# Fixed places for the transpositions between the output projection and the embedding's projection, whose results VectorE now takes out of PSUM

## The chip, the cores and the metric

The kernel is one program on one NeuronCore of a Trainium2 chip. Its time is the device time of one execution in microseconds (us). Five engines run their own instruction streams: PE (TensorE, matrix products, with its weight loads shown as PEld), DVE (VectorE), ACT (ScalarE), POOL (GpSimd) and SP (SyncE, which here only starts transfers). ACT and POOL can start transfers too. An engine works through its own stream in order, and waits where an instruction needs a result of another engine.

## The reference

One layer of a hybrid transformer on 512 tokens of width 1024, in float32. Two attentions (`nsa_mixer`, `moba_mixer`) give `y_nsa` and `y_moba`; after that:

```python
merged = sigmoid(gate_a) * (y_nsa @ w_up_nsa) + sigmoid(gate_b) * (y_moba @ w_up_moba)
x = x + merged @ w_out                                   # the output projection
gate, up = split(rms_norm(x, g_ffn) @ w_ffn_in, 2)       # the first feed-forward product
x = x + (silu(gate) * up) @ w_ffn_out
ple_gate = sigmoid(rms_norm(x, g_ple) @ w_ple_gate)
x = x + ple_gate * (p @ w_ple_proj)                      # p: an embedding of width 256 per token
```

The stage in question runs from the end of `merged @ w_out` to the first blocks of the feed-forward product. The embedding's projection `p @ w_ple_proj` depends on none of this; its result is needed only in the last line.

## The kernel before

**Precision.** Each float32 operand is split into a rounded high part and a low rest: ACT copies the high part (`wh`, L114 for weights; `x..h`, L1059 for activations), DVE subtracts it to get the low part (`wl`, L115; `x..l`, L1060). Each product is three matmuls: high by high, low by high, high by low (L1013, L1015, L1016 in the helper `mm`; L1132, L1134, L1135 in `in_product`). Weights arrive through SP's queue as pieces of 128x1024 (`wr`), which are numbered in the order of their use; `wh` and `wl` have four buffers each, taken in turn, so that piece 70 overwrites piece 66, and 71 overwrites 67.

**Output projection.** Eight PSUM tiles of 128 tokens x 512 columns: token tile `tt` = 0..3, column half `n` = 0, 1. They are named `wo<n><tt>`. Half of the contraction is done for all eight first; then, tile by tile, `wo_part` adds the second half (12 matmuls) and DVE adds the tile to the residual `X2[tt]` (L1073).

**Normalization and transposition.** When both column halves of two token tiles are done, `normed` takes the mean square of each row (ACT squares with a running sum, L1023; DVE scales, L1024; POOL raises to the power -1/2, L1025) and ACT scales the rows (L1027), giving `xs0`, `xs1` for the first pair of token tiles and `xs2`, `xs3` for the second. `turned_x` transposes them on PE (L1035): for each of four values of `u`, four 128x128 transpositions into one PSUM bank (`tx`), and ACT moves the bank to SBUF in two pieces with the gain `g_ffn` (`put_b`, L1064). The results are `B[k][c]`, k the half of the width, c the pair of token tiles: `B00`, `B10` come from the first pair, `B01`, `B11` from the second.

**Feed-forward product.** It is done by seven products per block instead of eight, on sums and differences of the four quarters. The operands are `x11` = B00, `x21` = B10, `x22` = B11, and `xt1`..`xt4`, which DVE forms from all four (L1096 to L1103). A block p does its products in an order of its own; in block 0 it is x11 (into bank `fx`), x21 (`fy`), xt1 (`fz`), xt2 (`fx` again, after ACT has copied it), then xt3, x22 and xt4. The weight pieces are 68 to 74 in block 0 and 75 to 81 in block 1; pieces 71 and 73 are sums that DVE forms in place (L106), of piece 70 with 68 and of that with 69.

**Embedding's projection.** `pj_part(n)` makes four tiles per column half (`pjb`, six matmuls each, weight pieces 66 and 67). ACT copies each to SBUF (`pps`, L1089) and starts its transfer to a DRAM buffer `ppd` (L1090), from which it is read back near the end.

**What sets the order.** The code is traced in the order in which it is written, and a scheduler then puts the instructions of each engine into an order of its own by a timeline that it estimates. `tc.issue_after(i)` ties the instructions of a block behind instruction `i` on its engine. The order below is what the scheduler made. PSUM has eight banks under four tags (`s`, `v`, `a`, `b`), two each; in the stage, the projection holds all eight, and `tx`, `pjb`, `fx`, `fy` and `fz` take them over as they come free.

Of the kernel before, what the change touches and what calls it, by code (L numbers as in the profile page):

```python
# [10 lines left out]
F32 = mybir.dt.float32  # L11
F32R = mybir.dt.float32r
I32 = mybir.dt.int32
AF = mybir.ActivationFunctionType
# [182 lines left out]
def hybrid_kernel(ctx: ExitStack, tc: tile.TileContext, a, out):  # L197
# [13 lines left out]
    def t4(name, dt=F32R):  # L211
        return big.tile([128, 2, 512], dt, name=name, tag="t4")

    def flat(t):
        return t.rearrange("p a b -> p (a b)")
# [795 lines left out]
    def mm(o, b, sth, stl, mh, ml, stop):  # L1011

        T.matmul(o, sth, mh, start=b.name not in seen, stop=False, skip_group_check=True)  # L1013
        seen.add(b.name)
        T.matmul(o, sth, ml, start=False, stop=False, skip_group_check=True)  # L1015
        T.matmul(o, stl, mh, start=False, stop=stop, skip_group_check=True)  # L1016

    def normed(c, name):

# [10 lines left out]
    def turned_x(xs, tag, put, us=range(4)):  # L1030
        for u in us:
            b = bank("tx", tag)
            for j in range(2):
                for i in range(2):
                    T.transpose(b[:, j * 256 + i * 128:j * 256 + i * 128 + 128],  # L1035
                                xs[i][:, (2 * u + j) * 128:(2 * u + j) * 128 + 128], ident)
            for j in range(2):
                put(2 * u + j, b[:, j * 256:j * 256 + 256])

    wob = [four("wo0", "sv"), four("wo1", "ab")]  # L1040

    def wo_part(n, u, w, tt):
        for j in range(2):
            kt = 2 * u + j
            mh, ml = (x[:, j * 512:(j + 1) * 512] for x in w)
            mm(wob[n][tt], wob[n][tt], MH[kt][:, tts(tt)], ML[kt][:, tts(tt)], mh, ml, kt == 7)

    for n in range(2):
        for u in range(2):
# [1 line left out]
            for tt in range(QT):  # L1051
                wo_part(n, u, w, tt)
    wn = [[W.get((f"wo{n}", u)) for u in (2, 3)] for n in range(2)]
    B = [[flat(t4(f"B{k}{c}", F32)) for c in range(2)] for k in range(2)]
    op = {}

    def split_x(nm, src):
        h, l = op[nm] = [flat(t4(f"x{nm}{x}")) for x in "hl"]
        A.activation(h, src, AF.Copy)  # L1059
        V.tensor_sub(l, src, h.bitcast(F32))  # L1060

    def put_b(c):
        def put(kt, src):
            A.activation(B[kt // 4][c][:, kt % 4 * 256:kt % 4 * 256 + 256], src, AF.Copy, scale=gv[:, 1, kt:kt + 1])  # L1064
        return put

    xs = [None, None]
    for tt in range(QT):
        for n in range(2):
            for u in (2, 3):  # L1070
                wo_part(n, u, wn[n][u - 2], tt)
            x = X2[tt][:, n * 512:(n + 1) * 512]
            V.scalar_tensor_tensor(x, wob[n][tt], 0.5, x, op0=OP.mult, op1=OP.add)  # L1073
        if tt % 2:
            xs[tt // 2] = normed(tt // 2, "xs")
        if tt == 2:
            turned_x(xs[0], "b", put_b(0))
            split_x("11", B[0][0])
            split_x("21", B[1][0])

    def pj_part(n):
        w = W.get(("pj", n))
        for tt in range(QT):
            b = bank("pjb", "va"[tt % 2])
            for kt in range(2):
                mh, ml = (x[:, kt * 512:(kt + 1) * 512] for x in w)
                mm(b, b, PIh[:, kt, tts(tt)], PIl[:, kt, tts(tt)], mh, ml, kt == 1)
            t = t2("pps")
            A.activation(t, b, AF.Copy)  # L1089
            A.dma_start(ppd[tt][:, n * 512:(n + 1) * 512], t)  # L1090

    pj_part(0)
    turned_x(xs[1], "b", put_b(1))
    pj_part(1)
    t1x, t2x = (flat(t4(f"x{nm}", F32)) for nm in ("t1", "t2"))
    V.tensor_tensor(t1x, B[0][0], B[0][1], op=OP.subtract)  # L1096
    split_x("t1", t1x)
# [262 lines left out]
```

## Time and profile before

| what | value |
|---|---|
| median of 3 runs | 844.34 us (843.9 to 844.61) |
| the profiled execution's own time | 842.11 us |
| its span, first to last instruction | 840.4 us |
| mean granted TensorE clock | 0.989 |
| PE busy | 818.4 us, 97% of the span |
| DVE busy | 620.1 us, 74% |
| ACT busy | 478.8 us, 57% |
| POOL busy | 144.6 us, 17% |

The span and what lies around it differ by 1.71 us. Times in the views count from the first instruction. A row of a timeline has the start, the duration (of a merged row, from its first start to its last end), engine, line, operation, tile written<-tiles read, shape, count, and in brackets the idle time before it with the instruction that ended it. Matmuls are pipelined: the duration of one is longer than the distance to the next. The granted clock (PEclk) is given as a share of full speed.

### The profile page before, as it was taken

How to read it: one execution, taken by the hardware profiler on the slowest of the kernel's cores; microseconds unless marked ns; L12 is line 12 of the kernel's file. 1: busy time of each engine (PE TensorE's matmuls, PEld its weight loads, DVE VectorE, ACT ScalarE, POOL GpSimd, SP SyncE). 2: the span in 40 equal slices, each digit the busy share in tenths (PEclk: the TensorE clock that was granted, in tenths of full speed). 3: DMA queues.
4: the chain of work that ended last, by engine and by line, in shares of the span. 5: the costliest groups of instructions: out<-in, count | busy, mean ns of one | idle time of the engine just before them, and what ended most of it. 6: DMA issues, size and time to landing. Idle time of an engine off the chain costs nothing.

```text
span 840.4 us, 12951 instructions
## 1 busy us (share of the span) xinstructions
PE 818.4 (97%) x4875; PEld 725.6 (86%) x4875; DVE 620.1 (74%) x1049; ACT 478.8 (57%) x823; POOL 144.6 (17%) x218
## 2 busy tenths in 40 slices
PE   9989999999999999999997999999999999999997
PEld 8869898788788888788885999999999988888776
DVE  7697758788977988739527877777778899966552
ACT  7434655876776767734448554544555644846441
POOL 3864426001111211007000111111120000000000
PEclk9989999999999999999998899999999999999999
DMA  9414554317888895234614367779998256577431
GB/s 346 153 58 131 164 142 126 101 51 217 230 223 208 236 270 144 76 101 168 207 39 162 114 236 275 279 238 271 275 273 247 76 151 205 155 222 210 175 147 51
DMA packets 40543, 150.31 MB, mean 179 GB/s; under 512 B 5153, under 2 KB 5537, under 8 KB 37921
## 3 DMA queue, kind: packets, MB, share of 16 engines
q1 hardware_dynamic: 30064, 98.61, 35.5%
q0 software_dynamic: 8064, 46.14, 21.6%
q10 hardware_dynamic: 2352, 4.73, 1.8%
q8 instruction: 38, 0.62, 0.3%
q14 instruction: 25, 0.20, 0.1%
HBM read 142.13 MB, written 50.33 MB: 229 GB/s over the span
## 4 chain that ended last, share of the span: by engine, by line
PE 87%; DVE 6%; ACT 3%; DMA 1%; issue 1%; POOL 0%; SPq 0%; ACTq 0%
PE fx L1132 5%; PE fx L1134 5%; PE fx L1135 5%; PE ga L412 3%; PE pt L834 3%; PE ga L414 3%; PE ga L413 3%; PE fz L1134 3%; PE fz L1135 3%; PE fz L1132 3%; PE fs L1016 2%; PE fs L1015 2%; PE fs L1013 2%; PE pv L858 2%; PE wo L1016 2%; PE wo L1015 2%
## 5 line engine op out<-in xcount | busy, mean ns | idle before, releaser
L114 ACT ACTIVATE wh<-wr 128x1024 fp32r<-128x1024 f32 (+2 forms) x196 | 199.0, 1021 | 177.6 <-issue 53.2
L115 DVE TENSOR_TENSOR wl<-wr,wh 128x1024 fp32r<-128x1024 f32 (+2 forms) x196 | 233.2, 1200 | 73.9 <-ACT wh L114 73.6
L412 PE MATMUL ga<-xh,wh 128*128 128x512 f32 x128 | 53.5, 418 | 0.0
L809 DVE CUSTOM_DVE_ANT_0 p<-sb,big_mask 128x512 f32<-128x512 f32 (+2 forms) x96 | 44.9, 486 | 9.1 <-PE sb L807 7.9
L413 PE MATMUL ga<-xl,wh 128*128 128x512 f32 x128 | 50.3, 393 | 0.0
L414 PE MATMUL ga<-xh,wl 128*128 128x512 f32 x128 | 50.1, 393 | 0.0
L834 PE MATMUL pt<-ident,p 128*128 128x128 f32 x240 | 38.3, 273 | 1.6 <-DVE pw L844 1.3
L844 DVE TENSOR_TENSOR pw<-pt,pw 128x512 fp32r<-128x512 f32 x48 | 32.7, 684 | 7.0 <-ACT pw L843 6.8
L1176 POOL COPY mark<-ks 128x1 f32<-128x1 f32 x11 | 7.9, 718 | 173.8 <-DVE ks L1146 173.8
L843 ACT ACTIVATE pw<-pt 128x512 fp32r<-128x512 f32 x48 | 28.0, 593 | 12.2 <-PE pt L834 11.8
L834 PEld LDWEIGHTS pt<-ident,p 128*128 128x128 f32 x240 | 28.9, 140 | 6.9 <-issue 1.4
L414 PEld LDWEIGHTS ga<-xh,wl 128*128 128x128 f32 x128 | 24.0, 188 | 5.3
L1132 PE MATMUL fz<-xt1h,wh 128*128 128x256 f32 x88 | 26.1, 297 | 1.9 <-ACT xt1h L1059 1.9
L1013 PE MATMUL pgb<-wh,x3h 128*128 128x512 f32 (+1 forms) x72 | 25.6, 372 | 1.8 <-ACT wh L114 1.2
L1134 PE MATMUL fz<-xt1l,wh 128*128 128x256 f32 x88 | 26.1, 297 | 0.9 <-DVE xt1l L1060 0.9
L413 PEld LDWEIGHTS ga<-xl,wh 128*128 128x128 f32 x128 | 24.2, 189 | 3.2
L106 DVE TENSOR_TENSOR wr<-wr,wr 128x1024 f32<-128x1024 f32 x22 | 26.8, 1220 | 0.1
L412 PEld LDWEIGHTS ga<-xh,wh 128*128 128x128 f32 x128 | 24.2, 189 | 3.1
L1015 PE MATMUL pgb<-wl,x3h 128*128 128x512 f32 (+1 forms) x72 | 25.8, 368 | 0.5 <-DVE wl L115 0.5
L1135 PE MATMUL fz<-xt1h,wl 128*128 128x256 f32 x88 | 26.0, 295 | 0.0
L1016 PE MATMUL pgb<-wh,x3l 128*128 128x512 f32 (+1 forms) x72 | 25.4, 368 | 0.0
L1132 PE MATMUL fx<-xt2h,wh 128*128 128x256 f32 x88 | 25.0, 284 | 0.0
(724 smaller groups left out, 2733.1 us busy)
## 6 DMA issues: line engine op xcount, KB each, us to landing
gs<-g POOLq DMA_DIRECT2D x20, 1024.0 KB, 8.9
wr<-g SPq DMA_DIRECT2D x33, 512.0 KB, 7.0
fs<-f POOLq DMA_DIRECT2D x24, 704.0 KB, 10.1
wr<-gs SPq DMA_DIRECT2D x22, 512.0 KB, 9.5
wr<-fs SPq DMA_DIRECT2D x20, 512.0 KB, 4.4
wr<-ga SPq DMA_DIRECT2D x16, 512.0 KB, 3.5
wr<-f SPq DMA_DIRECT2D x15, 512.0 KB, 3.7
fs<-fs POOLq DMA_DIRECT2D x8, 704.0 KB, 13.4
```

What stands on the lines that cost most here:

```text
L114: self.nc.scalar.activation(h[:, a:b], t[:, a:b], AF.Copy)
L115: self.nc.vector.tensor_sub(l[:, a:b], t[:, a:b], h[:, a:b].bitcast(F32))
L412: T.matmul(o, wh[:, sl], h, start=start, stop=False)
L413: T.matmul(o, wh[:, sl], l, start=False, stop=False)
L414: T.matmul(o, wl[:, sl], h, start=False, stop=stop)
L809: V.tensor_tensor_reduce(out=p, in0=o, in1=big_mask[:, 512 - n:512], op0=OP.add, op1=OP.min, scale=1.0, scalar=3.0e38, accum_out=st["m"][: ...
L834: last = T.transpose(b[:, off:off + 128], st["p"][:, P_OFF[qt] + kb * 128:P_OFF[qt] + kb * 128 + 128], ident)
L1015: T.matmul(o, sth, ml, start=False, stop=False, skip_group_check=True)
L1016: T.matmul(o, stl, mh, start=False, stop=stop, skip_group_check=True)
L1132: T.matmul(o, wh, xh, start=b.name not in seen, stop=False, skip_group_check=True)
L1134: T.matmul(o, wh, xl, start=False, stop=False, skip_group_check=True)
L1135: T.matmul(o, wl, xh, start=False, stop=kt == 3, skip_group_check=True)
```

## The change

The first pair's transpositions are written behind tiles (tt 2, n 1) and (tt 3, n 0) of the output projection, two values of `u` at each, and each next tile of the projection is tied behind the last transposition. They use the banks of tag `a`. All of column half 0 of the embedding's projection is tied behind the last matmul of the output projection. Of half 1 one tile comes next, then the second pair's transpositions for `u` 0 and 1, two tiles tied behind them, the transpositions for `u` 2 and 3, and the last tile tied behind those. The `pjb` banks are of tags `s` and `v`. DVE copies them to SBUF in place of ACT, and POOL's queue transfers them in place of ACT's. Each `B` tile is made when its first piece is written.

```diff
-        T.matmul(o, stl, mh, start=False, stop=stop, skip_group_check=True)
+        return T.matmul(o, stl, mh, start=False, stop=stop, skip_group_check=True).ins
...
-                    T.transpose(b[:, j * 256 + i * 128:j * 256 + i * 128 + 128],
-                                xs[i][:, (2 * u + j) * 128:(2 * u + j) * 128 + 128], ident)
+                    end = T.transpose(b[:, j * 256 + i * 128:j * 256 + i * 128 + 128],
+                                      xs[i][:, (2 * u + j) * 128:(2 * u + j) * 128 + 128], ident)
             for j in range(2):
                 put(2 * u + j, b[:, j * 256:j * 256 + 256])
+        return end.ins
...
-            mm(wob[n][tt], wob[n][tt], MH[kt][:, tts(tt)], ML[kt][:, tts(tt)], mh, ml, kt == 7)
+            end = mm(wob[n][tt], wob[n][tt], MH[kt][:, tts(tt)], ML[kt][:, tts(tt)], mh, ml, kt == 7)
+        return end
...
-    B = [[flat(t4(f"B{k}{c}", F32)) for c in range(2)] for k in range(2)]
+    B = [[None, None] for k in range(2)]
...
+            if kt % 4 == 0:
+                B[kt // 4][c] = flat(t4(f"B{kt // 4}{c}", F32))
...
+    turned_at = None
     for tt in range(QT):
         for n in range(2):
-            for u in (2, 3):
-                wo_part(n, u, wn[n][u - 2], tt)
+            with tc.issue_after(turned_at) if turned_at else nullcontext():
+                for u in (2, 3):
+                    last_wo = wo_part(n, u, wn[n][u - 2], tt)
             x = X2[tt][:, n * 512:(n + 1) * 512]
             V.scalar_tensor_tensor(x, wob[n][tt], 0.5, x, op0=OP.mult, op1=OP.add)
+            if (tt, n) in ((2, 1), (3, 0)):
+                turned_at = turned_x(xs[0], "a", put_b(0), (0, 1) if n else (2, 3))
+                if n == 0:
+                    split_x("11", B[0][0])
+                    split_x("21", B[1][0])
         if tt % 2:
             xs[tt // 2] = normed(tt // 2, "xs")
-        if tt == 2:
-            turned_x(xs[0], "b", put_b(0))
-            split_x("11", B[0][0])
-            split_x("21", B[1][0])
-
-    def pj_part(n):
-        w = W.get(("pj", n))
-        for tt in range(QT):
-            b = bank("pjb", "va"[tt % 2])
+
+    def pj_part(n, tts_):
+        w = wpj[n]
+        for tt in tts_:
+            b = bank("pjb", "sv"[tt % 2])
...
-            A.activation(t, b, AF.Copy)
-            A.dma_start(ppd[tt][:, n * 512:(n + 1) * 512], t)
-
-    pj_part(0)
-    turned_x(xs[1], "b", put_b(1))
-    pj_part(1)
+            V.tensor_copy(t, b)
+            G.dma_start(ppd[tt][:, n * 512:(n + 1) * 512], t)
+
+    wpj = [W.get(("pj", 0))]
+    with tc.issue_after(last_wo):
+        pj_part(0, range(4))
+    wpj.append(W.get(("pj", 1)))
+    pj_part(1, (0,))
+    at = turned_x(xs[1], "b", put_b(1), (0, 1))
+    with tc.issue_after(at):
+        pj_part(1, (1, 2))
+    at = turned_x(xs[1], "b", put_b(1), (2, 3))
+    with tc.issue_after(at):
+        pj_part(1, (3,))
```

In the new file the lines below L1035 have moved: L1064 is L1068, L1059 and L1060 are L1061 and L1062, L1089 is L1096, L1090 is L1097, L1096 to L1103 are L1111 to L1118, and L1132, L1134, L1135 are L1147, L1149, L1150.

**First place: PE, where the second pair is transposed.** Before, the sixteen transpositions of `xs2` (here `xs_4523`) and `xs3` (`xs_4524`) stand in one piece between the product of x21 and that of xt1:

```order
L1135 MATMUL fy<-x21h,wl_4680 128x256
L1035 MATMUL tx<-ident,xs_4523 128x128 x2
L1035 MATMUL tx<-ident,xs_4524 128x128
L1035 MATMUL tx<-ident,xs_4523 128x128
L1035 MATMUL tx<-ident,xs_4524 128x128 x2
...
L1132 MATMUL fz<-xt1h,wh_4709 128x256
L1134 MATMUL fz<-xt1l,wh_4709 128x256
```

Now (`xs_4521`, `xs_4522`) eight of them stand behind the fifth tile of the embedding's projection, and eight inside the product of x11, with the last tile behind them:

```order
L1016 MATMUL pjb<-wh_4529,PIl 128x512
L1035 MATMUL tx<-ident,xs_4521 128x128 x2
L1035 MATMUL tx<-ident,xs_4522 128x128
...
L1035 MATMUL tx<-ident,xs_4522 128x128
L1013 MATMUL pjb<-wh_4529,PIh 128x512
...
L1147 MATMUL fx<-x11h,wh_4573 128x256
L1035 MATMUL tx<-ident,xs_4521 128x128
L1035 MATMUL tx<-ident,xs_4522 128x128
```

Two tiles of the projection and ten matmuls of x11 lie between the two groups; the rest of x11, x21 and xt1 follow the last tile.

**Second place: ACT, ahead of the second pair's scaling.** Before, with the semaphores that each row waits for:

```order
L1089 ACTIVATE pps_4646<-pjb_4639 128x512 [waits DMAHW0_49,PE_49]
L114 ACTIVATE wh71_4744<-wr70_4365 128x1024 [waits DVE_49]
L1090 DMA ppd2_83<-pps_4636 128x512 [waits DMAHW5_49,Activation_49]
L1023 ACTIVATE xs2_4523,xs__4521<-X22_4203 128x1024 [waits DMAHW4_49]
L1023 ACTIVATE xs3_4524,xs__4521<-X23_4204 128x1024
L1090 DMA ppd3_84<-pps_4646 128x512 [waits Activation_49]
L114 ACTIVATE wh72_4776<-wr72_4607 128x1024 [waits DMAHW4_49,PE_49]
L1139 ACTIVATE kg11_4707<-fx_4676 128x512 [waits DMAHW1_49,PE_49]
L114 ACTIVATE wh73_4809<-wr70_4365 128x1024 [waits DVE_49,PE_49]
L1027 ACTIVATE xs2_4523<-X22_4203,xr__4522 128x1024 [waits Pool_49]
L1027 ACTIVATE xs3_4524<-X23_4204,xr__4522 128x1024 [waits Activation_49]
```

And now:

```order
L1061 ACTIVATE x21h_4502<-B10_4488 128x1024 [waits Activation_49]
L1023 ACTIVATE xs2_4521,xs__4519<-X22_4203 128x1024 [waits DMAHW4_49,DVE_49]
L1023 ACTIVATE xs3_4522,xs__4519<-X23_4204 128x1024 [waits DMAHW5_49,DVE_49]
L114 ACTIVATE wh70_4709<-wr70_4365 128x1024 [waits PE_49]
L1027 ACTIVATE xs2_4521<-X22_4203,xr__4520 128x1024 [waits Pool_49]
L1027 ACTIVATE xs3_4522<-X23_4204,xr__4520 128x1024 [waits Activation_49]
```

All eight copies `pps` and their transfers are gone from ACT, and one weight piece, number 70, is left between the squares and the scaling.

**Third place: DVE, from the operand xt1 to the low part of xt2.** Before, nothing stood between them but work on the same operands (xt1, B01, xt1l, xt2, B10, xt2l). Now:

```order
L1111 TENSOR_TENSOR xt1_4649<-B00_4460,B01_4594 128x1024 [waits Activation_49]
L1113 TENSOR_TENSOR B01_4594<-B11_4629,B01_4594 128x1024 [waits DVE_49,Activation_49]
L1096 COPY pps_4646<-pjb_4639 128x512 [waits DMASW2_49,PE_49]
L1062 TENSOR_TENSOR xt1l_4653<-xt1_4649,xt1h_4652 128x1024 [waits Activation_49]
L1114 SCALAR_TENSOR_TENSOR xt2_4650<-B00_4460,B01_4594 128x1024 [waits DVE_49]
L115 TENSOR_TENSOR wl71_4745<-wr70_4365,wh71_4744 128x1024 [waits Activation_49]
L115 TENSOR_TENSOR wl72_4777<-wr72_4577,wh72_4776 128x1024 [waits DMAHW4_49,PE_49,Activation_49]
L1118 SCALAR_TENSOR_TENSOR B10_4488<-xt2_4650,B10_4488 128x1024 [waits DVE_49]
L1159 TENSOR_TENSOR kg11_4707<-kg11_4707,fy_4677 128x512 [waits DMASW3_49,PE_49,Activation_49]
L1062 TENSOR_TENSOR xt2l_4659<-xt2_4650,xt2h_4658 128x1024 [waits Activation_49]
```

The copy of the last embedding tile, two weight pieces and an addition of the gate have come between. From the third block of the feed-forward product on, every engine but POOL has the order that it had, and POOL has its old order behind the eight transfers.

## The prediction

> **What bounds the kernel now.** I read the page's slices first: PE is busy in nearly all of them, and its clock dips right of the middle, in the stage of the change. The table by stretches, PE alone, shows how (columns: stretch, its length, PE busy and count of matmuls, granted clock, DMA share, GB/s):
>
> ```profile
> 428.00:451.94 23.94, 23.94 (x137) 1.00 0.33 111
> 451.94:457.15 5.21, 1.88 (x14) 1.00 0.78 245
> 457.15:467.41 10.26, 7.52 (x33) 0.50 0.08 31
> 467.41:501.73 34.32, 34.32 (x288) 1.00 0.56 193
> ```
>
> PE never waits before 451.94 nor after 467.41; in between it idles 3.33 + 2.74 = 6.07 us, and for 10.26 us runs at half clock. Its timeline says what it waits for:
>
> ```profile
> 427.99 0.39 PE L1013 MATMUL wo<-wh,MH 128*128 128x512 f32 x1
> ...
> 433.88 0.39 PE L1013 MATMUL pjb<-wh,PIh 128*128 128x512 f32 x1
> ...
> 438.92 1.03 PE L1035 MATMUL tx<-ident,xs 128*128 128x128 f32 x8
> ...
> 440.02 0.39 PE L1016 MATMUL pjb<-wh,PIl 128*128 128x512 f32 x1
> ...
> 451.82 0.28 PE L1135 MATMUL fy<-x21h,wl 128*128 128x256 f32 x1
> 454.24 0.44 PE L1035 MATMUL tx<-ident,xs 128*128 128x128 f32 x2 [2.13 <-ACT xs L1027]
> ...
> 460.47 0.58 PE L1132 MATMUL fz<-xt1h,wh 128*128 128x256 f32 x1 [1.87 <-ACT xt1h L1059]
> ...
> 501.73 0.28 PE L1132 MATMUL fz<-xt1h,wh 128*128 128x256 f32 x1
> 501.85 0.28 PE L1134 MATMUL fz<-xt1l,wh 128*128 128x256 f32 x1
> ```
>
> The second pair is scaled too late (454.24), its transpositions stand alone, and the operand xt1 follows them serially (460.47). The row at 501.73 opens xt1 in the third block; from there on the order is the old one, so I measure the change by when PE gets there.
>
> Unit prices from these rows: feed-forward matmul 501.85 - 501.73 = 0.12 us; eight transpositions 440.02 - 438.92, less the 0.23 of the matmul between, 0.87; 512-column matmul: 427.99 to 433.88 holds 24 of them and four transpositions (0.44), so 0.227.
>
> **The change part by part.** *The stage's loss.* From 451.94 to 467.41 are 15.47 us. Their work at full speed: sixteen transpositions 1.74, xt1's 24 matmuls 2.88, the first two of xt2 0.24, together 4.86. Lost: 10.6 us. That is the most the change can recover, since PE's work stays the same; what new waits take is to be subtracted. So I follow the new order.
>
> *First pair.* Its rows are scaled on ACT by 425.65 + 2.19 = 427.84 (first row below), just before PE gets to the new place at 427.99. Then: 24 matmuls of the projection 5.45 and sixteen transpositions 1.74; the embedding starts at 435.18, its half 0 ends at 440.63, its fifth tile at 441.99. The eight transpositions brought forward cost nothing more, only earlier. x11 and x21 are ready by 437, long before use.
>
> ACT's prices, from its timeline:
>
> ```profile
> 425.65 2.19 ACT L1027 ACTIVATE xs<-X,xr__4424 128x1024 f32<-128x1024 f32 x2 [1.03 <-POOL xr__4424 L1025]
> ...
> 439.55 1.57 ACT L1064 ACTIVATE B<-tx,gv 128x256 f32<-128x256 f32 x4 [0.75 <-PE tx L1035]
> ...
> 442.42 1.08 ACT L114 ACTIVATE wh<-wr 128x1024 fp32r<-128x1024 f32 x1
> 443.37 1.11 ACT L1089 ACTIVATE pps<-pjb 128x512 f32<-128x512 f32 x2
> ```
>
> DVE's one copy of this shape out of PSUM (ns: min/median/max; start), and its timeline:
>
> ```profile
> L389 DVE COPY rb<-st0c x1: 681/681/681, 32.9 to 32.9; 128x512 f32<-128x512 f32 x1
> ```
>
> ```profile
> 419.37 1.88 DVE L1073 SCALAR_TENSOR_TENSOR X<-wo,X 128x512 f32<-128x512 f32 x3
> ...
> 460.64 1.22 DVE L1060 TENSOR_TENSOR xt1l<-xt,xt1h 128x1024 fp32r<-128x1024 f32 x1
> 461.78 1.22 DVE L1099 SCALAR_TENSOR_TENSOR xt<-B,B 128x1024 f32<-128x1024 f32 x1
> ```
>
> On ACT a 1024-column piece keeps its successor off for 443.37 - 442.42 = 0.95; on DVE for 461.78 - 460.64 = 1.14, a 512-column one for (1.88 - 0.69) / 2 = 0.6. DVE's copy out of PSUM has one row, 0.68 alone; I take 0.6 in a row of work (0.68 at worst adds 0.1 to B below).
>
> *Wait A.* Before the second pair's scaling ACT now has weight piece 70, which overwrites piece 66 and so waits until PE has finished half 0 of the embedding: 440.63 - 0.23 + 0.39 = 440.79. Piece 70 then runs 440.83 to 441.78 (until its successor starts), `xs2` to 442.84, `xs3` to 443.97. Behind it on ACT stand only that scaling and the new evictions, and PE waits for them. PE is there at 441.99, does two transpositions (0.2) meanwhile, and goes on at 444.02: **A = 1.8 us**. The squares ahead of it are done by 438, so piece 70 ends last.
>
> Then six transpositions and two tiles (0.65 + 2.72) to 447.4, ten matmuls of x11 (1.2), eight transpositions to 449.5, last tile, 14 + 24 + 24 matmuls of x11, x21, xt1 (1.36 + 7.44) to 458.3.
>
> *Wait B.* The four last evictions end at 449.1 + 0.04 + 1.6 = 450.75. DVE then does B01, copy 8, xt1l, xt2, wl71, wl72, B10 and the gate's addition: six of 1.14 and two of 0.6, 8.0; xt2l runs 458.8 to 460.0. xt1l in this row is ready at 453.7, before PE's 455.5, so xt1 costs no wait any more. But PE wants xt2l at 458.4 and gets it at 460.1: **B = 1.7**. The old stall has moved from xt1 to xt2, and is smaller.
>
> *Wait C.* DVE's sum for piece 73 comes behind xt2l (460.0 to 461.2), then ACT splits 73, 74, 75 (0.95 each, 75 ready at 464.2) and copies xt2's bank (464.1 to 464.7). PE, in the order x22 (2 matmuls), x11 of block 1 (2), xt3, would be at xt3 at 460.1 + 27 x 0.12 = 463.3, and starts it at 464.7: **C = 1.4**. After it DVE leads PE by about 2 us at the closest place (low part of piece 78, wanted by the second block's x21), so I count nothing more.
>
> *VectorE instead of ScalarE.* Eight copies, 4.8 us, leave ACT (two in 1.11 in the row at 443.37) and enter DVE. Six lie where DVE would wait for PE; copy 8 is inside B (0.6).
>
> *POOL's queue instead of ACT's.* It removes ACT's issues. The first two transfers stand ahead of the power of -1/2, for which ACT's scaling waits:
>
> ```profile
> 451.38 0.70 POOL L1025 TENSOR_TENSOR xr__4522<-xs__4521,half_neg 128x2 f32<-128x2 f32 x1 [25.76 <-DVE xs__4521 L1024]
> ...
> 477.05 2.16 POOL L952 DMA_DIRECT2D fs<-f  x4
> ```
>
> An issue is 0.54, so the power ends at 438.8 + 0.6 + 0.7 = 440.1, and piece 70 covers it until 441.8; without that cover (issues over 1.4 each) A grows by the excess. The copies 6 to 8 reuse buffers of 1 to 3, so DVE waits for landings; the landing is bounded by these rows (KB each, median us from issue to landing):
>
> ```profile
> gs<-g POOLq DMA_DIRECT2D x4, 512.0 KB, 5.6
> ppd<-pps ACTq DMA_DIRECT2D x8, 256.0 KB, 2.0
> ```
>
> ```profile
> fs<-fs POOLq DMA_DIRECT2D x8, 704.0 KB, 13.4
> ```
>
> Between 2.0 and 13.4 I take at most 5.6, the same queue and the nearest size: issued at 438.4, landed by 444.0, wanted by copy 6 at 446.2. Cost nothing; 13.4 is a rival below. The Trainium skill ("DMA: Bandwidth & Descriptors", "SWDGE vs HWDGE vs iDMA") speaks against this move: GpSimd writes the descriptors of its transfers into SBUF and can be locked out there by VectorE's two-port modes, and transfers from ACT's queue cannot. By that rule A could grow; the row of four issues in 2.16 us, with DVE at work, shows nothing of it, and I go by the row.
>
> *Sum.* 10.6 - 1.8 - 1.7 - 1.4 = 5.7 us gained. Profiled execution: 840.4 - 5.7 = 834.7 span, 842.11 - 5.7 = 836.4. The runs' median lies 2.2 above the profiled one; I leave that difference as it is: 844.34 - 5.7 = **838.6 us**.
>
> **The rivals.** *The clock falls in A or B.* PE alone, stretches of 3.4 us cut where the granted clock changes:
>
> ```profile
> 47.56:50.98 3.42, 1.47 (x6) 1.00 0.02 5
> 50.98:54.38 3.40, 3.40 (x13) 0.50 0.45 154
> ```
>
> ```profile
> 450.32:453.74 3.42, 1.79 (x15) 1.00 0.60 193
> 453.74:457.15 3.41, 1.71 (x12) 1.00 0.82 265
> ```
>
> Busy shares of 43% (47.56) and 50% (453.74) were followed by half clock, 52% (450.32) was not. In A and in B, the last matmul's 0.28 to 0.39 taken off, PE idles about 1.5 us of such a stretch: busy some 55%, barely above. If one of them falls below, 3.4 us at half clock lose up to 1.7, two such stretches 3.4: 840.3 to 842.0. The Trainium skill ("TensorE: Matmul & The Clock Gate", "Why this matters for your kernels") warns of idle gaps over about 3 us; by that neither wait would trip it and the sum stands, but the 2 us gap inside 47.56 to 50.98 did, so I trust the rows.
>
> *Slower: POOL's transfers land late.* If each takes 13.4 us as the fs<-fs row, copy 6 waits until 451.8 and not 446.2, 5.6 late. Behind it on DVE stand xt1, xt1l and all the chain of B; PE has about 1 us of slack at xt1l, so it loses about 4.6 and further 1.3 as DVE's backlog reaches C: no gain left. Stalls of over 3 us then halve the clock for 3.4 to 6.8 us, 1.7 to 3.4 lost: 846 to 848. It decides from a landing of about 12 us. For it: same queue. Against it: those rows are nearly three times the size and accumulate, and the queue is empty here.
>
> *No change: the gain is given back.* DVE, 74% busy over the span, gets the copies. If its operations run longer beside PE's denser stream, the lead of 2 us at piece 78 is used up and PE waits once per product until DVE has caught up; about 4 us of slip would leave 843 to 845. Against it: no wait of PE in 34 us after 467.41, with the same weight pieces on DVE.
>
> *Better: A and C vanish*, if ACT's or DVE's order has slack that I don't see: 844.34 - 10.6 + 1.7 = 835.4.
>
> **How the numbers follow.** Forecast 0.54, clock 0.25, better 0.05, given back 0.10, late transfers 0.06. Of the forecast and the better case nearly all, and of the clock case most, is faster by over 0.2% (under 842.65; 0.2%, 1.7 us, is what a measurement of this kernel can tell from no change): 0.83. Given back is mostly within it, with the clock's worst: 0.10. Slower: 0.07. The forecast's own range is 837.2 to 840.3 (prices 0.1 to 0.3 off in A, B, C). With the clock case and a part of the better one, 8 in 10 lie in 835.8 to 842.8.
>
> **What would show it.** In the changed profile: no wait of PE for xt1h or xt1l; a wait of about 1.8 us in two pieces at `tx` for ACT's `xs` near 442 to 444; one of about 1.7 at `fx` for xt2l near 458 to 460; three small ones to 465; the clock at 1.00 from 428 to 500; xt1 of the third block at about 496.0 in place of 501.73. Wrong would be: half clock behind 444 or 460 (clock rival), a DVE wait for a landing of `ppd` (late transfers), PE waiting for `wl` between 470 and 500 (given back).

## The result, and the profile after

The changed kernel took 838.07 us (median of 4 runs, 835.84 to 838.91), the kernel before 844.48 beside it (4 runs): a ratio of 0.9921, 95% interval 0.9900 to 0.9942. Run again on another occasion it took 838.92 (6 runs, 837.11 to 840.21) against 842.90 (11 runs, 840.67 to 846.0): 0.9948, 0.9928 to 0.9968. One run of the kernel before in the last series below took 1003.88 us at a granted clock of 0.75; it is a slow run, and the ratios leave it out. The forecast was 838.6, in a range of 835.8 to 842.8.

PE alone in the changed kernel by stretches (columns: stretch, its length, PE busy and count of matmuls, granted clock, DMA share, GB/s):

```profile
426.65:440.80 14.15, 14.15 (x71) 1.00 0.13 50
440.80:443.50 2.70, 1.27 (x10) 1.00 0.35 135
443.50:457.20 13.70, 13.70 (x100) 1.00 0.37 119
457.20:459.20 2.00, 0.44 (x4) 1.00 0.69 240
459.20:463.60 4.40, 3.80 (x28) 1.00 0.41 119
463.60:494.78 31.18, 31.18 (x260) 1.00 0.61 215
```

The clock stays at 1.00 throughout, where before it was halved for 10.26 us. PE idles at three places instead of one. Its timeline names them:

```profile
426.65 1.03 PE L1035 MATMUL tx<-ident,xs 128*128 128x128 f32 x8
...
440.45 0.39 PE L1016 MATMUL pjb<-wh,PIl 128*128 128x512 f32 x1
441.67 0.44 PE L1035 MATMUL tx<-ident,xs 128*128 128x128 f32 x2 [0.83 <-ACT xs L1027]
442.71 0.33 PE L1035 MATMUL tx<-ident,xs 128*128 128x128 f32 x1 [0.60 <-ACT xs L1027]
...
457.05 0.28 PE L1147 MATMUL fx<-xt2h,wh 128*128 128x256 f32 x1
458.89 0.39 PE L1149 MATMUL fx<-xt2l,wh 128*128 128x256 f32 x1 [1.56 <-DVE xt2l L1062]
...
463.01 0.39 PE L1147 MATMUL fx<-x11h,wh 128*128 128x256 f32 x1 [0.33 <-ACT wh L114]
...
463.50 0.39 PE L1147 MATMUL fx<-xt3h,wh 128*128 128x256 f32 x1
...
494.78 0.28 PE L1147 MATMUL fz<-xt1h,wh 128*128 128x256 f32 x1
```

No row waits for xt1h or xt1l any more.

**A measure that the rest doesn't disturb.** I call the *stage* the time from PE's start behind tile (tt 2, n 1) of the output projection to its first matmul of xt1 in the third feed-forward block. Before, these are the rows 427.99 and 501.73 of the prediction: 73.74 us. After: 494.78 - 426.65 = 68.13. **The stage gained 5.61 us; 5.7 was forecast.**

The profiled execution as a whole went from a span of 840.4 to 834.1, by 6.3. The rest of that is not the stage: PE is at its start 1.34 us earlier (426.65 against 427.99), though no instruction ahead of it differs (the clock fell twice ahead of it before, once after), and 0.65 is lost again near the end, where PE waits for a weight piece whose transfer ACT waits for. Before, and after:

```profile
803.76 0.50 PE L1013 MATMUL pgb<-wh,x3h 128*128 128x512 f32 x1 [0.56 <-ACT wh L114]
```

```profile
797.48 1.35 PE L1013 MATMUL pgb<-wh,x3h 128*128 128x512 f32 x3 [1.21 <-ACT wh L114]
```

### The profile page after: what moved, and what is told of

It reads as the page before. It is cut to its first block, busy times and chain, and to the rows that moved or that the text cites. A ratio compares the mean times of both kernels' runs of the same rounds, so it can differ in the third digit from the quotient of the medians.

```text
span 834.1 us, 12951 instructions
## 1 busy us (share of the span) xinstructions
PE 813.2 (97%) x4875; PEld 721.1 (86%) x4875; DVE 624.1 (75%) x1057; ACT 474.7 (57%) x815; POOL 146.9 (18%) x226
## 4 chain that ended last, share of the span: by engine, by line
PE 89%; DVE 5%; ACT 3%; DMA 2%; issue 1%; SPq 0%; ACTq 0%
PE fx L1147 5%; PE fx L1149 5%; PE fx L1150 5%; PE ga L412 3%; PE pt L834 3%; PE ga L414 3%; PE ga L413 3%; PE fz L1150 2%; PE fz L1149 2%; PE fz L1147 2%; PE fs L1016 2%; PE fs L1013 2%; PE fs L1015 2%; PE wo L1015 2%; PE wo L1016 2%; PE wo L1013 2%
## 5 line engine op out<-in xcount | busy, mean ns | idle before, releaser
L1149 PE MATMUL fx<-xt2l,wh 128*128 128x256 f32 x88 | 25.0, 284 | 1.6 <-DVE xt2l L1062 1.6
L1147 PE MATMUL fx<-x11h,wh 128*128 128x256 f32 x88 | 25.0, 284 | 0.3 <-ACT wh L114 0.3
L1149 PE MATMUL fz<-x22l,wh 128*128 128x256 f32 x88 | 25.0, 284 | 0.3 <-DVE x22l L1062 0.3
L1013 PE MATMUL wo<-wh,MH 128*128 128x512 f32 x64 | 25.1, 392 | 0.0
```

Of the source, the lines that this page charges most:

```text
L1147: T.matmul(o, wh, xh, start=b.name not in seen, stop=False, skip_group_check=True)
L1149: T.matmul(o, wh, xl, start=False, stop=False, skip_group_check=True)
```

## The experiments

Stage and times of all runs. Each ratio is against the kernel before in the same series (medians there: 844.48 beside the first changed row, 842.90 beside the next four, 843.57 from "before again" to "first pair only", 843.37 for the last four). Of the stage there is one trace per row.

| run | stage, us | median, us (runs) | ratio, 95% interval |
|---|---|---|---|
| before | 73.74 | 844.48 (4) | |
| changed | 68.13 | 838.07 (4) | 0.9921, 0.9900 to 0.9942 |
| changed again | 68.14 | 838.92 (6) | 0.9948, 0.9928 to 0.9968 |
| scaling first (no A) | 67.06 | 837.73 (6) | 0.9937, 0.9919 to 0.9955 |
| xt2l first (no B) | 67.70 | 837.45 (6) | 0.9938, 0.9916 to 0.9959 |
| both | 66.48 | 835.60 (6) | 0.9910, 0.9890 to 0.9930 |
| before again | 73.74 | 843.04 (10) | 1.0004, 0.9988 to 1.0019 |
| copies only | 72.88 | 842.69 (10) | 0.9993, 0.9975 to 1.0010 |
| copies on ACT | 68.29 | 837.28 (10) | 0.9937, 0.9918 to 0.9955 |
| first pair only | 68.54 | 837.62 (4) | 0.9936, 0.9914 to 0.9958 |
| ACT's queue | 66.48 | 835.30 (4) | 0.9900, 0.9875 to 0.9925 |
| second pair only | 76.23 | 845.91 (10) | 1.0034, 1.0019 to 1.0049 |
| longer wait A | 69.18 | 839.18 (10) | 0.9956, 0.9938 to 0.9975 |
| all waits | 64.30 | 834.10 (6) | 0.9892, 0.9869 to 0.9914 |

### Both kernels once more

No edit. For the changed kernel:

> The changed kernel once more, for a second trace of it and more of its times. Its runs so far lie between 835.84 and 838.91 us, at mean clocks of 0.998 to 0.993. Theory 1 (the spread comes from outside the stage, from stretches of half clock elsewhere): the stage, from the first transposition of the first pair to the first matmul of xt1 in the third block, takes 68.1 us again (494.78 - 426.65) with the clock at 1.00 in it. Rival (the clock falls in wait A or B in some executions): a trace of a longer execution shows half clock behind 444 or 460, and the stage 69.8 to 71.5.

For the kernel before:

> The kernel before once more, for a second trace. The stage, from the place behind tile (tt 2, n 1) of the output projection to the first matmul of xt1 in the third block, took 73.74 us (501.73 - 427.99) in the first trace and 68.13 in the changed kernel's two. Theory 1: the waits of PE are the same ones (xs, xt1h, xt1l), and the stage comes out between 72 and 75.4 by where the stretches of half clock fall on them (3.4 us of half clock more or less are 1.7 us). Rival: the stage is 73.7 to 0.1, and all spread between runs is from elsewhere. And: if the wait of PE at pgb for the weight piece (0.56 us before, 1.21 in the changed kernel's traces) is a matter of the transfers and not of the change, it can come out at 1.2 here too.

Both stages came out the same to 0.01 us, 68.14 and 73.74, with the same waits. For the changed kernel theory 1 holds: its two traced executions took 835.84 and 838.90, and the 3.1 us between them do not come from the stage. For the kernel before the rival holds as far as the traces go: they are of 842.11 and 842.67 us, and none of its longer runs (up to 846.17) was traced. The stage starts at 429.49 in the second trace of the changed kernel and at 426.65 in the first; the clock fell three times ahead of it there, against once. That is not the only source: in the run with xt2l first, below, the clock fell once too, and the stage starts at 429.00, behind longer waits of PE near 50 and 60 us (3.04 and 2.80, in the first trace 2.81 and 1.57). Therefore the stage is what I compare below; the medians carry a noise of 1 to 2 us.

The wait at pgb in the second trace of the kernel before:

```profile
804.30 1.35 PE L1013 MATMUL pgb<-wh,x3h 128*128 128x512 f32 x3 [0.66 <-ACT wh L114]
```

It was 0.56 and 0.66 before, 1.21 and 1.17 in the changed kernel's two traces, and 0.64 to 1.06 in the other runs. Whether the change does it stays open: no run was made on that place.

### Are A, B and C separate terms?

Piece 70 behind the second pair's scaling (wait A):

```diff
-            A.activation(xs[i], X2[2 * c + i], AF.Copy, scale=rn[:, i:i + 1])
+            scaled[:] = [A.activation(xs[i], X2[2 * c + i], AF.Copy, scale=rn[:, i:i + 1]).ins]
...
-        w = W.get((key, p))
+        with tc.issue_after(tied[key]) if p == 0 and key in tied else nullcontext():
+            w = W.get((key, p))          # tied = dict(g12=scaled[0])
```

> Piece 70 is tied behind the scaling of the second pair on ACT, which takes wait A away and nothing else (the last tile's copy on DVE and two or three rows move by one place). Theory 1 (A is a loss of its own): the scaling can start when POOL's power is done, 439.2, and ends at 441.4; PE, there at 440.65, loses 0 to 0.3 instead of 1.7, everything behind comes 1.5 earlier, and B and C stay as they are: stage 66.6 in place of 68.1, time 1.5 below the changed kernel's, about 836.5. Rival (VectorE's chain is what bounds, and A only hides it): xt2l is no earlier than now, B grows by what A loses, stage 68.1, time as the changed kernel's, 838.1.

xt2l ahead of B10 and of the low part of piece 72 (wait B):

```diff
+    with tc.issue_after(low2):           # low2: the subtraction that gives xt2l
         V.scalar_tensor_tensor(B[1][0], t2x, -1.0, B[1][0], op0=OP.mult, op1=OP.subtract)
...
+        with tc.issue_after(tied[key]) if p == 0 and key in tied else nullcontext():
+            w = W.get((key, p))          # tied = dict(s2=low2)
```

> On DVE the low part of piece 72, B10 and what hangs on it are tied behind xt2l, which takes about 2 us from ahead of it; A stays. Theory 1 (B and C are separate terms, as in the sum of the prediction): B's 1.6 vanishes, C stays at about 0.8: stage 66.5, time about 836.5. Rival (B and C are one backlog of DVE and ACT behind the second pair's evictions; the order only chooses which product waits): no wait for xt2l, but 0.8 each for the copy of xt2's bank, for piece 73 and for piece 76, stage 67.5, time 0.6 below the changed kernel's, 837.4.

Both together:

> Both edits of the two runs before: piece 70 behind the second pair's scaling on ACT, and xt2l ahead of B10 and the low part of piece 72 on DVE. Theory 1 (A, B and C add up): 1.5 and 1.6 gained, stage 65.0, time 835.0. Rival (A is separate, B and C are one backlog): 1.5 and 0.7 gained, stage 65.9, time 835.8. Rival (the backlog takes it all): stage 68.1, 838.1.

Without A the stage is 67.06, 1.07 shorter. ACT's and PE's rows with the scaling first:

```profile
442.50 2.19 ACT L1029 ACTIVATE xs<-X,xr__4520 128x1024 f32<-128x1024 f32 x2 [2.64 <-POOL xr__4520 L1027]
```

```profile
444.74 0.87 PE L1037 MATMUL tx<-ident,xs 128*128 128x128 f32 x6 [0.41 <-ACT xs L1029]
...
461.08 0.39 PE L1154 MATMUL fx<-xt2l,wh 128*128 128x256 f32 x1 [1.66 <-DVE xt2l L1064]
```

A is a loss of its own, as theory 1 had it: B grew only from 1.56 to 1.66. But 0.41 us of A is left (I had expected 0 to 0.3), and ACT now waits for POOL's power and not for PE. The run on ACT's queue below takes this up.

With xt2l first the stage is 67.70, 0.43 shorter, and not 1.6: theory 1 falls. B is gone, and three waits have come in its place:

```profile
463.12 0.38 PE L1151 MATMUL fx<-xt3h,wh 128*128 128x256 f32 x1 [0.69 <-ACT ks L1158]
464.07 0.38 PE L1151 MATMUL fz<-x22h,wh 128*128 128x256 f32 x1 [0.56 <-ACT wh L114]
...
468.29 0.39 PE L1151 MATMUL fz<-xt1h,wh 128*128 128x256 f32 x1 [0.73 <-ACT wh L114]
```

Together 1.98 us, in place of B and C's 1.56 + 0.27 + 0.33 = 2.16. In the changed kernel B and C do have one source, as DVE's stretches there show:

```profile
435.80:449.61 13.81, 8.33 (x13) 1.00 0.48 171
449.61:467.90 18.29, 18.29 (x18) 1.00 0.33 98
```

From the last eviction on (449.61) DVE works without a gap for 18.29 us, and xt2l, the sum for piece 73 and the low part of x22 stand in that row. But the three new waits are not simply this backlog moved to other products. The rival had named all three (0.8 each) and put them down to a backlog of DVE and ACT; each is ended by ACT, and ahead of two of them ACT itself stood idle and waited for PE:

```profile
462.47 0.60 ACT L1158 ACTIVATE ks<-fx 128x512 f32<-128x512 f32 x1 [1.33 <-PE fx L1154]
...
467.18 1.06 ACT L114 ACTIVATE wh<-wr 128x1024 fp32r<-128x1024 f32 x1 [1.27 <-PE fx L1153]
```

In this order PE has xt3 right behind xt2, so it waits until ACT has emptied the bank `fx`, which both use. Piece 73 is split behind that copy, and piece 76 waits until PE is done with the buffer of piece 72. So the rival's 67.5 was nearly met, but its reason holds only in part. Both edits give 66.48, 1.65 less than the changed kernel: about the sum of 1.07 and 0.43, as the first rival of that run said in kind (it gave 2.2).

### Which part of the change carries the gain?

The copies alone, in the kernel before (PE's order is untouched):

```diff
-            A.activation(t, b, AF.Copy)
-            A.dma_start(ppd[tt][:, n * 512:(n + 1) * 512], t)
+            V.tensor_copy(t, b)
+            G.dma_start(ppd[tt][:, n * 512:(n + 1) * 512], t)
```

> Only the copies on DVE and POOL's queue, the transpositions' places as before; PE's order is that of the kernel before, row for row, and ACT's loses the copies and has piece 73 behind the second pair's scaling. Theory 1 (the places make the gain): the second pair is scaled 1.9 us earlier, but its transpositions still stand alone, and PE still waits for the evictions, xt1h and xt1l (1.75 + 2.08 + 1.23): at full clock the stage would be 70.6, and with the clock falling in such stretches 1.7 to 3.4 more, 72.3 to 74: 0 to 1.5 of the 5.6. Rival (relieving ACT makes the gain): stage 68.1 to 69.5, 4 us or more.

The reverse edit, in the changed kernel:

> The new places, but the copies on ACT and their transfers on ACT's queue as before. ACT then has copies 1 and 2 and no weight piece ahead of the second pair's scaling, piece 70 goes behind it, and DVE's sum for piece 73 comes ahead of xt2l. Theory 1 (the places make the gain, the engine of the copies only moves the waits): no wait A; PE waits about 3.0 for xt2l and 2.1 for piece 73's low part: stage 68.3 if the clock holds, 70 if it falls once. Rival (the move to DVE is needed for the gain): stage 71.5 or more, PE waiting for xs or xt1 as before.

The first pair's places alone (with the copies on DVE; the scheduler puts the second pair where it likes):

```diff
     with tc.issue_after(last_wo):
         pj_part(0, range(4))
+    turned_x(xs[1], "b", put_b(1))
     wpj.append(W.get(("pj", 1)))
-    pj_part(1, (0,))
-    at = turned_x(xs[1], "b", put_b(1), (0, 1))
-    with tc.issue_after(at):
-        pj_part(1, (1, 2))
-    at = turned_x(xs[1], "b", put_b(1), (2, 3))
-    with tc.issue_after(at):
-        pj_part(1, (3,))
+    with tc.issue_after(last_wo):
+        pj_part(1, range(4))
```

> The first pair's places and the copies on DVE as in the change, the embedding's half 0 behind the projection; the second pair's transpositions and half 1 are written one behind the other as before and left to the scheduler, which spreads the sixteen over the products of x11 and x21 and puts half 1 ahead of them. Theory 1 (the second pair's places are what keeps xt1 from being late): PE waits 2.1 for xt1h, 1.6 for xt1l and 1.1 for xt2l; at full clock that would still be a stage of 68.1, since no wait A stands ahead; but 3.7 us of idleness within 6 halve the clock, and the stage is 69.8 to 71.5. Rival (the first pair's places are all that matters): no wait for xt1, clock at 1.00, stage 68.1 or less.

The second pair's places alone (with the copies on DVE):

```diff
-            if (tt, n) in ((2, 1), (3, 0)):
-                turned_at = turned_x(xs[0], "a", put_b(0), (0, 1) if n else (2, 3))
-                if n == 0:
-                    split_x("11", B[0][0])
-                    split_x("21", B[1][0])
         if tt % 2:
             xs[tt // 2] = normed(tt // 2, "xs")
+        if tt == 2:
+            turned_x(xs[0], "b", put_b(0))
+            split_x("11", B[0][0])
+            split_x("21", B[1][0])
```

> The second pair's places, the ties of half 1 and the copies on DVE as in the change; the first pair's transpositions are written as before, behind the projection, and lie among the embedding's half 0. Theory 1 (the first pair's places are what lets ACT get to the second pair in time, and the ties alone make PE wait for it): x11h, x21h and the squares come late, xs2 is scaled only near 447.8 on the changed kernel's clock, and PE, tied to the transpositions, waits 7.2 us for it in one piece, then 0.9, and later for xt2l about 1.4: stage 73.8 at full clock, and with one or two stretches of half clock behind such a wait 75.5 to 77.2: slower than before (73.7). Rival (the second pair's places carry the gain, as the run with the first pair's places alone seemed to leave room for): stage 69 or less.

The copies alone take 0.86 off the stage (72.88): ACT scales the second pair sooner, and PE waits for the transpositions and for xt1 as before.

```profile
451.63 0.44 PE L1035 MATMUL tx<-ident,xs 128*128 128x128 f32 x2 [0.99 <-ACT xs L1027]
...
458.70 0.58 PE L1132 MATMUL fz<-xt1h,wh 128*128 128x256 f32 x1 [1.88 <-ACT xt1h L1059]
```

Conversely, with the new places and the copies left on ACT the stage is 68.29: 0.16 from the changed kernel's. Wait A is gone there, and the wait for xt2l is longer:

```profile
458.86 0.39 PE L1149 MATMUL fx<-xt2l,wh 128*128 128x256 f32 x1 [2.80 <-DVE xt2l L1062]
```

On balance the engine of the copies is worth next to nothing with the new places; the places make the gain, as theory 1 had it in both runs.

The first pair's places alone, with the copies moved, bring 5.2 of the 5.6 (68.54); against the copies alone it is 4.3. The second pair did not stay where it was, though: left to the scheduler, its transpositions stand at 446.81, 447.99, 451.64 and 452.43, which is 18 to 24 us behind the start of the stage and not 26 to 29 as before, and PE waits for none of them. So the run shows that the second pair hardly needs ties of its own once the first is early, and not that its place has no effect. Theory 1 of that run had 69.8 to 71.5 and is wrong in the sum, though its waits and the clock are there:

```profile
456.44 0.38 PE L1143 MATMUL fz<-xt1h,wh 128*128 128x256 f32 x1 [1.98 <-ACT xt1h L1061]
458.34 0.39 PE L1145 MATMUL fz<-xt1l,wh 128*128 128x256 f32 x1 [1.52 <-DVE xt1l L1062]
```

```profile
455.17:458.58 3.41, 0.62 (x3) 1.00 0.43 125
458.58:462.00 3.42, 3.42 (x18) 0.50 0.36 137
```

At half clock PE has no wait for xt2l, which I had put at 1.1 there. By that layout it lost little by the 3.4 us of half clock: it would have waited for DVE anyway. With the copies on ACT the same is to be seen: the clock is halved from 459.68 to 463.09, and the wait for piece 73's low part is 0.40 in place of the 2.1 expected.

The second pair's places alone make the kernel slower than before: stage 76.23, +2.5, ratio 1.0034 (1.0019 to 1.0049). PE is tied to the transpositions and waits for the scaling, which ACT reaches late because x11h and x21h come late:

```profile
451.17 0.69 PE L1035 MATMUL tx<-ident,xs 128*128 128x128 f32 x2 [6.94 <-ACT xs L1027]
```

```profile
446.87:450.28 3.41, 0.00 (x0) 0.50 0.33 89
450.28:453.69 3.41, 2.17 (x9) 0.50 0.16 65
453.69:457.10 3.41, 3.41 (x10) 0.50 0.00 0
```

Theory 1 gave 75.5 to 77.2 and a wait of 7.2.

### What POOL's queue costs

```diff
-            G.dma_start(ppd[tt][:, n * 512:(n + 1) * 512], t)
+            A.dma_start(ppd[tt][:, n * 512:(n + 1) * 512], t)
```

> The change with the eight transfers on ACT's queue in place of POOL's; the copies stay on DVE. ACT's order then has piece 70 behind the second pair's scaling, as in the run with the scaling first, and POOL's power of -1/2 has no issues ahead of it. Theory 1 (with A's cover gone, POOL's two issues ahead of the power, 1.1 us, are what was left of wait A there, 0.41 us): no wait at the transpositions at all, stage 66.6 to 66.7, 0.4 below that run's 67.06. Rival (POOL's queue costs nothing on the path): 67.06 again. Theory 1 holds too that B then grows by what A loses beyond what VectorE can follow, by 0.1 to 0.4.

POOL in the changed kernel, and then with ACT's queue:

```profile
437.90 0.56 POOL L1097 DMA_DIRECT2D ppd<-pps  x1 [0.38 <-DVE xs__4519 L1024]
438.48 0.72 POOL L1025 TENSOR_TENSOR xr__4520<-xs__4519,half_neg 128x2 f32<-128x2 f32 x1
```

```profile
440.06 0.70 POOL L1025 TENSOR_TENSOR xr__4520<-xs__4519,half_neg 128x2 f32<-128x2 f32 x1 [13.36 <-DVE xs__4519 L1024]
```

From the start of the stage the power starts at 438.48 - 426.65 = 11.83 us in the one (11.83 too in the run with the scaling first) and at 440.06 - 429.07 = 10.99 in the other. PE's second pair then waits for nothing:

```profile
443.10 1.03 PE L1035 MATMUL tx<-ident,xs 128*128 128x128 f32 x8
```

The stage is 66.48, 0.58 below the run with the scaling first; 0.4 was expected. C's two waits are the same in both runs (0.28 and 0.33), and B is 1.76 in place of 1.66. What went with the two issues is the wait at the transpositions: 0.41 us of idle time, for which the third one came 0.68 us behind the second, and not 0.11 as here. So POOL's queue costs about 0.6 us as soon as piece 70 doesn't hide it.

### The clock gate, tried

The scaling of xs2 done twice, the second time to the same result, lengthens wait A:

```diff
-        for i in range(2):
+        for i in (0, 0, 1) if (c, name) == (1, "xs") else (0, 1):
             A.activation(xs[i], X2[2 * c + i], AF.Copy, scale=rn[:, i:i + 1])
```

> The change with the scaling of xs2 done twice (the same numbers again), so that wait A is 1.04 us longer and comes in one piece of about 3.1 us. In all traces so far the clock was halved behind stretches of 3.41 us in which the matmuls' own streaming time (distance to the next one, at most the duration less the 0.16 us by which a lone one is longer) filled under 0.43 of the stretch, and never above 0.48; A and B of the changed kernel reach 0.49 at least. Theory 1 (it is that share that decides): with 3.1 us of idleness the share falls under 0.3, the clock halves for 3.41 us behind about 445 on the changed kernel's clock, and the stage is 68.13 + 1.04 + up to 1.7, 70 to 70.9. Rival (a wait of about 3 us doesn't halve the clock): clock at 1.00, stage 69.2.

```profile
443.71 1.09 PE L1035 MATMUL tx<-ident,xs 128*128 128x128 f32 x8 [2.91 <-ACT xs L1027]
```

```profile
439.06:442.47 3.41, 1.75 (x8) 1.00 0.57 222
442.47:445.89 3.42, 2.18 (x14) 1.00 0.51 144
445.89:449.30 3.41, 3.41 (x25) 1.00 0.41 163
```

The wait is 2.91 us in one piece, the clock stays at 1.00, and the stage is 69.18, as the rival had it. The wait happens to lie across two stretches of the grid described in the last section, 51% and 64% busy, so this trace can't tell a rule on the length of the wait from one on the share of a stretch: by the count of that section the emptier of the two is filled to 0.46, and not under 0.3 as theory 1 had taken it. The kernel's ten runs spread widely (836.28 to 843.15, at clocks of 0.998 to 0.991), but those with the copies on ACT do so nearly as much (834.95 to 841.75). A clock that falls in some of them would fit; no trace of such a run was taken.

### A version against all three waits

Both ties of the earlier runs, ACT's queue, and further:

```diff
-            V.tensor_copy(t, b)
+            if (n, tt) in ((1, 3),):
+                A.activation(t, b, AF.Copy)
+            else:
+                V.tensor_copy(t, b)
...
+        if p == 0 and key in ('g22',):
+            tied[key] = kept_ins["ks2"]  # the copy of xt2's bank, ahead of piece 75
```

> A version against all three waits: the scaling of the second pair ahead of piece 70 and the transfers on ACT's queue (A), xt2l ahead of B10 and of the low part of piece 72, and the last embedding tile copied by ACT in place of DVE (B), the copy of xt2's bank ahead of piece 75 (C). By the rows of the changed kernel laid end to end in the new order: no wait A, 0.2 for xt2l, 0.7 for the copy of xt2's bank: stage 64.1, 4.0 below the changed kernel; the last runs of this kind came out 0.2 to 0.6 less good than so laid out, so 64.2 to 64.9 and a time near 834.5 to 835.5. Rival (VectorE's and ACT's backlog behind the second pair's evictions bounds, and every order of it loses about 2.5 us, as with both edits of the earlier run, stage 66.5): 66 or more, 836 or more.

```profile
430.59:494.89 64.30, 63.62 (x465) 1.00 0.50 168
```

The stage is 64.30, within 64.2 to 64.9: 3.83 below the changed kernel and 9.4 below the kernel before. The rival, 66 or more, falls. One wait of 0.6 us is left, for the copy of xt2's bank, the same handover of `fx` as with xt2l first. Beside the run with ACT's queue (66.48) this one has three more edits, the tie of xt2l, one copy of 0.6 us taken from DVE, and the copy of xt2's bank ahead of piece 75 (that of piece 70 only fixes the order that the run had); together they brought 2.18 us, and which of them did how much was not measured. The median of 6 runs is 834.10 us (834.5 to 835.5 was expected), a ratio of 0.9892 (0.9869 to 0.9914) to the kernel before. The changed kernel was not run beside it; that this one is faster rests on the stage. The edit to ACT's queue alone, one word, has 0.9900 (0.9875 to 0.9925).

## Why the prediction was right

- **The stage's loss, 10.6.** The trace repeats it: 73.74 us twice, with the same rows.
- **First pair.** The start of the transpositions at the new place had no wait, and x11 and x21 cost none, as worked out.
- **Wait A, 1.8.** Without it the third transposition would have stood at 440.90 (the last projection matmul at 440.45, 0.23 for it and 0.22 for two transpositions); it stood at 442.71: 1.81. In the row of ACT, piece 70 waits 2.92 us for PE and ends just ahead of the scaling:

```profile
439.52 1.06 ACT L114 ACTIVATE wh<-wr 128x1024 fp32r<-128x1024 f32 x1 [2.92 <-PE pjb L1016]
440.48 1.13 ACT L1027 ACTIVATE xs<-X,xr__4520 128x1024 f32<-128x1024 f32 x1
```

- **Wait B, 1.7.** 458.89 - 457.05 - 0.12 = 1.72.
- **Wait C, 1.4.** From xt2l 27 matmuls to xt3 would be 3.24; 463.50 - 458.89 = 4.61: 1.37. It did not end where it was laid out: the prediction let the copy of xt2's bank end it, and in the profile PE waits for the low part of x22 on DVE (0.27), which the sum doesn't name, and for a weight piece on ACT (0.33); behind these the copy costs 0.15.
- **The sum, 5.7.** 10.6 - 1.81 - 1.72 - 1.37 = 5.7; the stage gained 5.61. Where the terms stand was right, and so was what ends A and B. What the runs don't bear out is how the sum treats B and C: as two terms with causes of their own. In the changed kernel both follow from the one row of DVE without a gap, and the order that took B away had waits of its own, so that it gave 0.43 and not 1.7. The sum was right because the order was given and laid out operation by operation. (That PE never waits after 467.41 holds in the stage alone: it waits at 803.76.)
- **VectorE for ScalarE.** Copies took 0.69 each, 0.61 in a row of work, as taken (0.6). That the engine matters little is shown by both runs on it.
- **POOL's queue, "cost nothing".** The cover named for it, piece 70, was the right one. The prediction thought of losing it only by longer issues (over 1.4 us); with the cover itself taken away, issues of 0.56 to 0.65 cost 0.6. The transfers landed after 2.3 us (5.6 was allowed for), so the rival of late landings had no ground. The Trainium skill ("DMA: Bandwidth & Descriptors", "SWDGE vs HWDGE vs iDMA") warns that VectorE's two-port modes can hold up GpSimd's descriptors; with POOL's queue beside a busy DVE no issue here took over 0.65 us. Whether DVE was in such a mode then, no run shows. What POOL's queue cost came from its place ahead of the power.
- **The clock.** It held in A and B, in both traces. The reason given, a threshold between 50% and 52% of PE's busy time, is wrong (last section).
- **The median.** The forecast took the profiled difference to the median of the runs shown, 844.34 - 5.7. The changed kernel's medians in the two series differ from it by -0.5 and +0.3, less than the 1 to 2 us by which half clock and waits ahead of the stage move any of them; beside their own kernel before they are 6.4 and 4.0 lower. That the median came so near is in part luck; the 5.61 of the stage is not.

## What to carry to other kernels

A transposition, or any step that a chain of other engines hangs on, belongs where its input is ready and other work still stands behind it; but tying PE to it pays only once the input really is early: here, with the copies on DVE, the first pair's places gained 5.2 us, and the second pair's, without these, lost 2.5. When an engine works without a gap behind the point of a wait, taking that one wait away can return only a part (0.43 of 1.7), and the new order has to be read for waits of its own: two of the three here were handovers between PE and ACT. To compare versions by fractions of a per cent, measure from a fixed instruction ahead of the change to one behind it in the trace: in two traces of each kernel this repeated to 0.01 us, where the runs' times spread by 3 to 5.

## What was not expected of the hardware

**Half clock comes on a fixed grid.** In the first trace before, it begins at 50.97, 61.20 and 457.15: 457.15 - 50.97 = 119 x 3.413. All traces agree with one length of 3.41 us for a stretch. The Trainium skill ("TensorE: Matmul & The Clock Gate", "What's actually happening") states a free-running window of 3413 ns, and the traces agree with it.

**PE's busy share doesn't decide.** In the run with xt2l first:

```profile
49.14:52.56 3.42, 1.64 (x7) 1.00 0.02 5
...
226.64:230.05 3.41, 2.03 (x10) 1.00 0.77 284
230.05:233.46 3.41, 3.15 (x12) 0.50 0.98 348
```

48% busy was not followed by half clock, 60% was. A lone matmul's row is longer than its share of a stream (0.39 against 0.227 for 512 columns), so many short bursts look busier than they are. I counted for each matmul the distance to the next, at most its duration less 0.16. By this count, in the 14 traces, of the stretches at full clock all 18 under 0.40 were followed by half clock, none above 0.47 was, and between them both happened. At half clock it takes more: stretches up to 0.70 were followed by another at half clock, those from 0.83 on were not. That is a description of these traces, with the phase of the grid taken from the rows; why it is not sharp stays open. The same skill page ("Why this matters for your kernels") puts the limit at idle gaps of over about 3 us; here a gap of 2.03 us was followed by half clock (in the stretch 47.56 to 50.98 of the prediction), and one of 2.91 was not, nor one of 3.12 that ends at 51.6 in the version against all three waits.

**Half clock can cost little.** In two runs 3.4 us of it lay where PE, by the layout, would have waited for DVE anyway, and the stages (68.29 and 68.54) were within 0.5 us of what was laid out at full clock (68.3 and 68.1). No run had the same order at full clock there, so this is argued and not shown.
